# Seven block products for eight in a part of the feed-forward products of a hybrid decoder layer

## The chip, the cores and the metric

The kernel runs on one core of a Trainium2 chip. The metric is the device time of one launch in microseconds (us), the median of the runs shown. Where a profiled execution is quoted, its times count from the start of its span.

## What is computed

One layer on 256 tokens of width 2048, all in float32: a feed-forward half step (FFN1, 5632 inner columns), a mixing step (one input projection, a causal convolution over 31 taps, differential attention, one output projection), cross-attention into 256 memory tokens, and a second feed-forward half step (FFN2). Cut to what matters here:

```python
def rms_norm(x, g):
    xf = x.astype(jnp.float32)
    y = xf * lax.rsqrt(jnp.mean(xf * xf, axis=-1, keepdims=True) + EPS)
    return (y * g.astype(jnp.float32)).astype(x.dtype)

def swiglu(h, w_gate, w_up, w_down):
    return (jax.nn.silu(h @ w_gate) * (h @ w_up)) @ w_down
...
        x = x + 0.5 * swiglu(rms_norm(x, ffn1_norm_g[l]), ffn1_w_gate[l], ffn1_w_up[l], ffn1_w_down[l])
        h = rms_norm(x, mix_norm_g[l])
        p = h @ w_in[l]
...
        x = x + jnp.concatenate([o_diff, o_conv], axis=-1) @ w_out[l]
        x = x + memory_cross_attention(rms_norm(x, xattn_norm_g[l]), rms_norm(mem, mem_norm_g[l]),
                                       xattn_w_q[l], xattn_w_kv[l],
                                       xattn_q_norm_g[l], xattn_k_norm_g[l], xattn_w_o[l])
        x = x + 0.5 * swiglu(rms_norm(x, ffn2_norm_g[l]), ffn2_w_gate[l], ffn2_w_up[l], ffn2_w_down[l])
```

## The kernel before

**A weight product.** TensorE multiplies at reduced precision, so every float32 operand is split in two parts: hi (a rounded copy, `h`) and lo (what is left, `l`). A product of 128 rows of weights takes three passes, hi x hi (line 186), hi x lo (187) and lo x hi (189). Tokens are the stationary operand (two blocks of 128, `tb`), 512 columns of weights the moving one.

**A quad.** `proj` goes through two column slices (`j`) and both token blocks at once, in four accumulators of 128 x 512 in PSUM (`acc00` to `acc11`). It takes the weights in pairs of 128-row tiles. Per pair: one transfer of 512 KB per column slice (line 172, issued on SyncE's queue), a split of each (line 136, the cast on ScalarE; line 137, the subtraction on VectorE), and 2 x 2 x 2 x 3 = 24 products. In the last pair of a quad each accumulator's products stand together, so that the accumulators end one after the other, and `evac` empties them. The raw weights have 4 buffers, `wh` and `wl` 5 each, in one pool `wp` for the whole program: when TensorE has used a tile, the next split may start, and the one after it is loaded.

**Feed-forward.** The 5632 inner columns are 11 slices of 512, in groups of 4, 4 and 3. Per slice there is one *in-quad* (gate and up are the two column slices, 16 row tiles, so 8 pairs), then silu (line 289, ScalarE) and the multiplication to `h` (291, VectorE). Two steps later (`later(2, turn)`) TensorE transposes `h` (297), and it is split again into `hth` (299) and `htl` (300). After a group come two *down-quads*, each over 1024 of the 2048 output columns, 8 pairs in a group of four and 6 in the group of three; their sums are added to x (line 311).

**Between phases.** When a column group of x is final, ScalarE squares it (197), TensorE transposes it 8 times (208, a *turn*), ScalarE scales the result with the gains (`xh`, 211) and VectorE takes the lo part (`xl`, 212). A turn is put off by one or two weight steps with `later`.

**Memory tokens.** `mem_group` loads 512 columns of the memory, squares them, loads them transposed, and splits them with the gains: `mh` (218, ScalarE) and `ml` (219, VectorE), 16 of each. It is done in FFN1, at weight steps 12, 18, 24 and 30.

**Order.** Each engine runs its queue in order. The order within a queue is set at build time by a scheduler that follows the program order with the priorities and estimates it has; `later` and `behind` steer it. Convolution taps (721, 724) fill VectorE's queue wherever there is room in mixing.

## Time and profile before

| | |
|---|---|
| median of 3 runs | 1926.21 us (1925.92 to 1926.83) |
| span of the profiled execution | 1923.9 us |
| TensorE (PE) busy | 1911.3 us, 99% |
| VectorE (DVE) busy | 1095.0 us, 57% |
| ScalarE (ACT) busy | 879.1 us, 46% |
| transferred | 364.70 MB, 190 GB/s |

The span is that of one execution under the profiler; about 2.3 us lie around it. FFN1 fills it to 741, mixing to about 1060, cross-attention to 1190, FFN2 the rest. A row of the timeline is: start, duration, engine, line of the kernel, operation, what it writes and reads, and in brackets how long the engine stood idle before and what released it. Matmuls are pipelined: what one costs is the distance between starts, not its duration.

### The profile page before, as it was taken

To read this page: it belongs to the slowest core of one execution; us is meant where nothing else is said; L and a number is where in the kernel's file an instruction comes from. 1 tells how busy PE (TensorE), PEld (TensorE's weight loads), DVE (VectorE), ACT (ScalarE), POOL (GpSimd) and SP (SyncE) were. 2 spreads that over 40 slices of the span, in tenths; PEclk is the share of its full clock that TensorE was granted. 3 is DMA by queue.
4 is the path that set the end of the run, shared out by engine and by line. 5 is a ranking of instruction groups with operands and counts; after the bars stand their busy time and mean duration, and the time that the engine had idled before them with its cause. 6 is when DMAs were issued, how large, how long until landed. Compare 5 with 4: busy or idle time off the path is not lost.

```text
span 1923.9 us, 22869 instructions
## 1 busy us (share of the span) xinstructions
PE 1911.3 (99%) x8650; PEld 1579.1 (82%) x8650; DVE 1095.0 (57%) x1430; ACT 879.1 (46%) x1173; POOL 20.7 (1%) x29
## 2 busy tenths in 40 slices
...
GB/s 297 257 211 200 192 196 186 187 196 187 190 193 195 188 185 182 190 190 189 171 129 129 198 177 144 185 196 187 186 196 197 188 185 195 193 187 190 195 186 155
DMA packets 188815, 364.70 MB, mean 190 GB/s; under 512 B 11680, under 2 KB 12192, under 8 KB 188704
## 3 DMA queue, kind: packets, MB, share of 16 engines
...
HBM read 361.09 MB, written 2.10 MB: 189 GB/s over the span
## 4 chain that ended last, share of the span: by engine, by line
PE 87%; DVE 8%; DMA 2%; issue 1%; ACT 1%; POOL 0%; SPq 0%; DVEq 0%; ACTq 0%
PE acc L186 28%; PE acc L189 28%; PE acc L187 28%; DVE y L724 3%; DVE wl L137 3%; PE tp L297 1%; DMA raw<-ffn_w_up 1%; DMA raw<-ffn_w_gate 1%; PE tp L208 1%; ACT wh L136 1%; DMA raw<-w_out 0%; DVE nb L591 0%; DVE qms L536 0%; DVE uT L741 0%; DVE uT L730 0%
## 5 line engine op out<-in xcount | busy, mean ns | idle before, releaser
L137 DVE TENSOR_TENSOR wl<-raw,wh 128x1024 fp32r<-128x1024 f32 (+1 forms) x674 | 800.7, 1217 | 759.1 <-ACT wh L136 757.8
L136 ACT CAST wh<-raw 128x1024 fp32r<-128x1024 f32 (+1 forms) x674 | 682.2, 1049 | 953.3 <-PE acc L189 917.0
L186 PE MATMUL acc<-wh,xh_f 128*128 128x512 f32 x1408 | 550.5, 392 | 2.3 <-ACT s L289 2.0
L187 PE MATMUL acc<-wl,xh_f 128*128 128x512 f32 x1408 | 549.0, 390 | 0.5 <-DVE wl L137 0.4
L189 PE MATMUL acc<-wh,xl_f 128*128 128x512 f32 x1408 | 450.1, 390 | 0.0
L186 PEld LDWEIGHTS acc<-wh,xh_f 128*128 128x128 f32 x1408 | 264.9, 188 | 58.4 <-ACT s L289 2.4
L187 PEld LDWEIGHTS acc<-wl,xh_f 128*128 128x128 f32 x1408 | 265.0, 188 | 56.3 <-DVE wl L137 2.1
L189 PEld LDWEIGHTS acc<-wh,xl_f 128*128 128x128 f32 x1408 | 264.6, 188 | 55.0
L186 PE MATMUL acc<-wh,hth 128*128 128x512 f32 x704 | 274.8, 390 | 0.0
L187 PE MATMUL acc<-wl,hth 128*128 128x512 f32 x704 | 273.9, 389 | 0.0
L189 PE MATMUL acc<-wh,htl 128*128 128x512 f32 x704 | 224.6, 389 | 0.0
L189 PEld LDWEIGHTS acc<-wh,htl 128*128 128x128 f32 x704 | 132.1, 188 | 27.5
L186 PEld LDWEIGHTS acc<-wh,hth 128*128 128x128 f32 x704 | 132.2, 188 | 27.2
L187 PEld LDWEIGHTS acc<-wl,hth 128*128 128x128 f32 x704 | 132.2, 188 | 27.1
L186 PE MATMUL acc<-wh,xh_mix 128*128 128x512 f32 x320 | 125.4, 392 | 0.0
L187 PE MATMUL acc<-wl,xh_mix 128*128 128x512 f32 x320 | 124.6, 389 | 0.0
L189 PE MATMUL acc<-wh,xl_mix 128*128 128x512 f32 x320 | 101.9, 389 | 0.0
L724 DVE SCALAR_TENSOR_TENSOR y<-uT,cw,y 128x256 f32<-128x256 f32 x240 | 100.6, 469 | 0.1
L189 PEld LDWEIGHTS acc<-wh,xl_mix 128*128 128x128 f32 x320 | 60.1, 188 | 12.6
L186 PEld LDWEIGHTS acc<-wh,xh_mix 128*128 128x128 f32 x320 | 60.1, 188 | 12.3
L187 PEld LDWEIGHTS acc<-wl,xh_mix 128*128 128x128 f32 x320 | 60.1, 188 | 12.1
L291 DVE SCALAR_TENSOR_TENSOR h<-acc,rstd_f,s 128x512 f32<-128x512 f32 x44 | 32.8, 748 | 33.1 <-PE acc L189 32.0
...
## 6 DMA issues: line engine op xcount, KB each, us to landing
...
```

The source lines that it names most:

```text
L136: last[:] = [S.copy(out=wh, in_=raw), V.tensor_tensor(out=wl, in0=raw, in1=wh.bitcast(F32), op=ALU.subtract)]
L137: V.tensor_tensor(out=wl, in0=raw, in1=wh.bitcast(F32), op=ALU.subtract)]
L186: T.matmul(acc[tb][j], hs, wt[k, j][0], start=(fresh and k == 0), stop=False)
L187: T.matmul(acc[tb][j], hs, wt[k, j][1], start=False, stop=False)
L189: T.matmul(acc[tb][j], ls, wt[k, j][0], start=False, stop=(ending and k == nk - 1))
L208: T.transpose(tp[:, b, tb * P:(tb + 1) * P], srcs[tb][:, c * P:(c + 1) * P], ident)
L291: V.scalar_tensor_tensor(out=h, in0=acc[1], scalar=norm.rs(tb), in1=s, op0=ALU.mult, op1=ALU.mult)
L297: T.transpose(tp[:, i, :], h[:, i * P:(i + 1) * P], ident)
L724: V.scalar_tensor_tensor(out=yc, in0=u[:, j:j + 256], scalar=cw[:, j * 8 + ct:j * 8 + ct + 1], in1=yc, op0=ALU.mult, op1=ALU.add)
```

## The change

Two (or one) of the pairs of a feed-forward quad are computed in the manner of Strassen's scheme as Winograd arranged it. Seen as blocks, a pair is a product of a 2 x 2 matrix of token blocks (two token blocks, two 128-row tiles) with a 2 x 2 matrix of weights (two row tiles, two column slices): eight block products. In a *seven pair* there are seven, each with its three passes, so 21 matmuls for 24. They need sums of weights (lines 245, 247, 248, written over the raw weights, then split like weights: four pairs of `wh`/`wl` tiles instead of two, one of them half used) and sums of tokens (`token_sums`: four subtractions of 128 x 128, a cast `sh` and a subtraction `sl`). Two of the products go only into extra PSUM tiles (`p1`, `q6`, in the two banks of `tpp` used for transposes) and two into `q57`, two banks that the attention's pool `atp` had for the whole program and that are now opened per phase. After the last seven pair of a quad, `middle` combines them (`p1s`, `us`, `vw`, and `ys` in in-quads). In an in-quad, each accumulator is then added to its share (`full`, line 441) before silu and `h`; in a down-quad the shares are added to x directly (line 476, five operations).

Seven pairs are: pairs 1 and 3 of all in-quads but the very first; in the down-quads two pairs in groups of four (positions 3 and 5 of the order) and one in groups of three (position 3). There are 42 + 20 = 62 of them. The transposes of `h` come seven steps later instead of two, but for the last slice of a group.

The weight pool is made per phase: `wf` in the feed-forward (3 raw tiles of 1 MB, each for one pair of both column slices, 7 of `wh` and `wl`), `wm` in between with the sizes of before. The memory's preparation moves into mixing, to its weight steps 6, 12, 18 and 24. The sums for the normalised x (`row_sums`, copies at line 317) are made with the turns.

```diff
+RAWS, SPLITS = 3, 7
+S_IN = (1, 3)
+ORDER_0 = tuple(range(8))
+ORDER_IN = (0, 1, 2, 3, 4, 5, 6, 7)
+S_DOWN = {4: 2, 3: 1}
+ORDER_DOWN = {4: (1, 3, 4, 0, 5, 2, 6, 7), 3: (1, 3, 2, 0, 4, 5)}
...
-    wp = ctx.enter_context(tc.tile_pool(name="wp", bufs=5))
     xtp = ctx.enter_context(tc.tile_pool(name="xtp", bufs=4))
+    xsp = ctx.enter_context(tc.tile_pool(name="xsp", bufs=len(S_IN)))
-    atp = ctx.enter_context(tc.tile_pool(name="atp", bufs=2, space=PSUM))
...
+    def passes(acc, hs, ls, w, start, stop):
+        T.matmul(acc, hs, w[0], start=start, stop=False)
+        T.matmul(acc, hs, w[1], start=False, stop=False)
+        T.matmul(acc, ls, w[0], start=False, stop=stop)
+    def quad(parts, srcs, middle, evac, first=False):
+        acc = [[accp.tile([P, 512], F32, tag=f"acc{tb}{j}", name=f"acc{tb}{j}") for j in range(2)]
+               for tb in range(2)]
+        begun = set()
+        seven = [i for i, p in enumerate(parts) if p()[4]]
+        q = None
+        for n, part in enumerate(parts):
+            h, l, i0, row, sums = part()
+            raw = ph["w"].tile([P, 4, 512], F32, tag="raw", name="raw", bufs=RAWS)
+            wa, wb = split_tiles(), split_tiles()
...
+                nc.sync.dma_start(out=raw[:, 0:4:3, :], in_=rows_pair(srcs[0], row))
+                nc.sync.dma_start(out=raw[:, 1:3, :], in_=rows_pair(srcs[1], row))
+                split(raw[:, 0:2, :], *wa)
+                if sums:
+                    split(raw[:, 3, :], wb[0][:, 1, :], wb[1][:, 1, :])
+                else:
+                    split(raw[:, 2:4, :], *wb)
+            ev0, ev1, od1, od0 = [tuple(t[:, c, :] for t in w) for w in (wa, wb) for c in range(2)]
+            def at(b, tb):
+                return [t[:, i0 + b, tb * P:(tb + 1) * P] for t in (h, l)]
+            if sums:
+                V.tensor_tensor(out=raw[:, 1:3, :], in0=raw[:, 1:3, :], in1=raw[:, 2:4, :], op=ALU.add)
+                V.tensor_tensor(out=raw[:, 3, :], in0=raw[:, 3, :], in1=raw[:, 1, :], op=ALU.add)
+                V.tensor_tensor(out=raw[:, 0, :], in0=raw[:, 0, :], in1=raw[:, 3, :], op=ALU.add)
+                wc, wd = split_tiles(), split_tiles()
+                split(raw[:, 1:3, :], *wc)
+                split(raw[:, 0:4:3, :], *wd)
+                t3, t1, t4, t2 = [tuple(t[:, c, :] for t in w) for w in (wc, wd) for c in range(2)]
+                sh, sl = sums
+                def s(c):
+                    return [t[:, c, :] for t in (sh, sl)]
+                if q is None:
+                    q = {"p1": tpp.tile([P, 512], F32, tag="tp", name="p1"),
+                         "q6": tpp.tile([P, 512], F32, tag="tp", name="q6"),
+                         "q57": ph["q"].tile([P, 2, 512], F32, tag="q57", name="q57")}
+                st, sp = n == seven[0], n == seven[-1]
+                passes(acc[0][0], *at(0, 0), ev0, "00" not in begun, False)
+                passes(acc[0][1], *s(3), ev1, "01" not in begun, False)
+                passes(q["p1"], *at(1, 0), od0, st, sp)
+                passes(q["q57"][:, 1, :], *s(2), t3, st, sp)
+                passes(q["q57"][:, 0, :], *s(0), t1, st, sp)
+                passes(acc[1][0], *at(0, 1), t4, "10" not in begun, False)
+                passes(q["q6"], *s(1), t2, st, sp)
+                begun |= {"00", "01", "10"}
+                if sp:
+                    middle(q)
+            else:
+                ending = n == len(parts) - 1
+                wt = [[ev0, ev1], [od0, od1]]
+                for tb in range(2):
+                    for js in ([[0], [1]] if ending else [[0, 1]]):
+                        for b in range(2):
+                            hs, ls = at(b, tb)
+                            for j in js:
+                                T.matmul(acc[tb][j], hs, wt[b][j][0], start=f"{tb}{j}" not in begun, stop=False)
+                                begun.add(f"{tb}{j}")
+                                T.matmul(acc[tb][j], hs, wt[b][j][1], start=False, stop=False)
+                            for j in js:
+                                T.matmul(acc[tb][j], ls, wt[b][j][0], start=False, stop=(ending and b == 1))
+                    if ending:
+                        evac(tb, acc[tb])
+            step()
...
+    def combine(q, pool):
+        p1 = pool.tile([P, 512], F32, tag="p1", name="p1s", bufs=1)
+        S.copy(out=p1, in_=q["p1"])
+        u = pool.tile([P, 512], F32, tag="u", name="us", bufs=1)
+        V.tensor_tensor(out=u, in0=q["q6"], in1=p1, op=ALU.subtract)
+        vw = pool.tile([P, 2, 512], F32, tag="vw", name="vw", bufs=1)
+        V.tensor_tensor(out=vw, in0=q["q57"], in1=u.unsqueeze(1).broadcast_to([P, 2, 512]), op=ALU.add)
+        return p1, vw
+    def token_sums(pool, bufs, o0, e0, o1, e1):
+        s = ph["f"].tile([P, 4, P], F32, tag="sraw", name="sraw", bufs=1)
+        V.tensor_tensor(out=s[:, 0, :], in0=o1, in1=e1, op=ALU.subtract)
+        V.tensor_tensor(out=s[:, 2, :], in0=o1, in1=o0, op=ALU.subtract)
+        V.tensor_tensor(out=s[:, 1, :], in0=o0, in1=s[:, 0, :], op=ALU.subtract)
+        V.tensor_tensor(out=s[:, 3, :], in0=e0, in1=s[:, 1, :], op=ALU.subtract)
+        sh = pool.tile([P, 4, P], F32R, tag="sh", name="sh", bufs=bufs)
+        sl = pool.tile([P, 4, P], F32R, tag="sl", name="sl", bufs=bufs)
+        S.copy(out=sh, in_=s)
+        V.tensor_tensor(out=sl, in0=s, in1=sh.bitcast(F32), op=ALU.subtract)
+        return sh, sl
+    def row_sums(raws, g):
+        f = ph["f"].tile([P, 2, 256], F32, tag="xsf", name="xsf", bufs=1)
+        for c in range(2):
+            S.activation(out=f[:, c, :], in_=raws[c], func=AF.Copy, scale=col(g + c))
+        return token_sums(xsp, len(S_IN), f[:, 1, 0:P], f[:, 0, 0:P], f[:, 1, P:], f[:, 0, P:])
...
+            if pair:
+                pair(a, tp)
...
+        def pair(self, i, raws):
+            if i in self.wanted:
+                self.sums[i] = row_sums(raws, self.g0 + 2 * i)
+        def parts(self, order, seven):
+            return [lambda i=i: (*(self.grp[i // 2] or (None, None)), 2 * (i % 2), 2 * i,
+                                 i in seven and self.sums.get(i, True)) for i in order]
...
+        with tc.tile_pool(name="wf", bufs=SPLITS, reuse_waits="tile") as wf, \
+                tc.tile_pool(name="ffn", bufs=2, reuse_waits="tile") as fp, \
+                tc.tile_pool(name="qp", bufs=1, space=PSUM) as qp:
+            ph.update(w=wf, f=fp, q=qp)
...
+                    def middle(q, rest=rest):
+                        p1, vw = combine(q, fp)
+                        y = fp.tile([P, 512], F32, tag="y", name="ys", bufs=1)
+                        V.tensor_tensor(out=y, in0=vw[:, 0, :], in1=q["q57"][:, 1, :], op=ALU.add)
+                        rest.update({(0, 0): (p1, ALU.add), (0, 1): (vw[:, 0, :], ALU.add),
+                                     (1, 0): (vw[:, 1, :], ALU.subtract), (1, 1): (y, ALU.add)})
+                    def evac(tb, acc, c=c, rest=rest, end=(c == c0 + ng - 1), pairs=(c - c0 < s_down)):
+                        acc = list(acc)
+                        for j in range(2):
+                            if rest:
+                                t = fp.tile([P, 512], F32, tag="full", name="full")
+                                V.tensor_tensor(out=t, in0=acc[j], in1=rest[tb, j][0], op=rest[tb, j][1])
+                                acc[j] = t
...
-                        later(2, turn)
+                            if pairs:
+                                if tb == 0:
+                                    hold[c] = fp.tile([P, 2, 2, P], F32, tag="hold", name="hold", bufs=1)
+                                f = hold[c]
+                                S.copy(out=f[:, tb], in_=tp[:, 0:2, :])
+                                if tb:
+                                    hsums[c] = token_sums(fp, max(S_DOWN.values()), f[:, 0, 1, :], f[:, 0, 0, :],
+                                                          f[:, 1, 1, :], f[:, 1, 0, :])
+                        later(2 if end else 7, turn)
+                    quad(norm.parts(ORDER_0 if start else ORDER_IN, sevens),
+                         [wg[:, c * 512:(c + 1) * 512], wu[:, c * 512:(c + 1) * 512]], middle, evac, first=start)
...
+                    def middle(q, n0=n0):
+                        p1, vw = combine(q, fp)
+                        for tb, j, t, f in ((0, 0, p1, 0.5), (0, 1, vw[:, 0, :], 0.5), (1, 0, vw[:, 1, :], -0.5),
+                                            (1, 1, vw[:, 0, :], 0.5), (1, 1, q["q57"][:, 1, :], 0.5)):
+                            xt = X[tb][n0 + j]
...
-                    kst = [(hts[c][0], hts[c][1], i, c * 4 + i) for c in range(c0, c0 + ng) for i in range(4)]
-                    proj(kst, [wd[:, n * 512:(n + 1) * 512] for n in (n0, n0 + 1)], evac)
+                    parts = [lambda c=c0 + i // 2, a=i % 2, i=i: (*hts[c], 2 * a, c * 4 + 2 * a,
+                                                                  a == 0 and i // 2 < s_down and hsums[c])
+                             for i in ORDER_DOWN[ng]]
+                    quad(parts, [wd[:, n * 512:(n + 1) * 512] for n in (n0, n0 + 1)], middle, evac)
...
+        n1.pair(i, [raw[:, c, :] for c in range(2)])
...
-    memp = ctx.enter_context(tc.tile_pool(name="memp", bufs=1))
+    mids = ctx.enter_context(ExitStack())
+    ph["w"] = mids.enter_context(tc.tile_pool(name="wm", bufs=5, reuse_waits="tile"))
+    memp = mids.enter_context(tc.tile_pool(name="memp", bufs=1, reuse_waits="tile"))
+    atp = mids.enter_context(tc.tile_pool(name="atp", bufs=2, space=PSUM))
...
+        m = ph["w"].tile([P, 2, 512], F32, tag="raw", name="memraw", bufs=4)
+        nc.sync.dma_start(out=m, in_=mem[:, n * 512:(n + 1) * 512].rearrange("(b p) n -> p b n", p=P))
...
-        later(12 + 6 * n, lambda n=n: mem_group(n))
+        later(6 + 6 * n, lambda n=n: mem_group(n))
...
+    mids.close()
```

**VectorE, one in-quad of FFN2.** `wl` are the subtractions of the split, `h` and `htl` as above. Before:

```order
682 L137 TENSOR_TENSOR wl<-raw,wh 128x1024 x13
683 L291 SCALAR_TENSOR_TENSOR h<-acc_13934,rstd_f_9641,s 128x512
684 L291 SCALAR_TENSOR_TENSOR h<-acc_13936,rstd_f_9641,s 128x512
685 L137 TENSOR_TENSOR wl<-raw,wh 128x1024 x3
686 L300 TENSOR_TENSOR htl<-tp,hth 128x4x128 x2
```

After, the end of an in-quad and the start of the next with its first seven pair:

```order
1057 L441 TENSOR_TENSOR full<-acc_11145,vw 128x512
1058 L446 SCALAR_TENSOR_TENSOR h<-full,rstd_f_10142,s 128x512
1059 L441 TENSOR_TENSOR full<-acc_11146,vw 128x512
1060 L441 TENSOR_TENSOR full<-acc_11147,ys 128x512
1061 L150 TENSOR_TENSOR wl<-raw,wh 128x1024
1062 L446 SCALAR_TENSOR_TENSOR h<-full,rstd_f_10142,s 128x512
1063 L150 TENSOR_TENSOR wl<-raw,wh 128x1024
1064 L245 TENSOR_TENSOR raw<-raw 128x1024
1065 L150 TENSOR_TENSOR wl<-raw,wh 128x512
1066 L247 TENSOR_TENSOR raw<-raw 128x512
1067 L248 TENSOR_TENSOR raw<-raw 128x512
1068 L150 TENSOR_TENSOR wl<-raw,wh 128x1024
```

The 13 and 3 subtractions of a quad have got the adds of the weights and of the accumulators among them; each `h` stands behind the two `full` of its token block.

**ScalarE, the program's start.** `xh` are the rows of x times the gains, the casts of 512 the first pair's weights in halves, those of 1024 the next pair's. Before:

```order
6 L136 CAST wh<-raw 128x512 x2
7 L218 ACTIVATE xh_f_108<-x_78,gT 128x256 x2
8 L136 CAST wh<-raw 128x1024 x2
9 L218 ACTIVATE xh_f_110<-x_82,gT 128x256 x2
10 L136 CAST wh<-raw 128x1024 x2
```

After:

```order
6 L149 CAST wh<-raw 128x512 x2
7 L345 ACTIVATE xh_f_105<-x_75,gT 128x256 x2
8 L317 ACTIVATE xsf<-x_75,gT 128x256 x2
9 L309 CAST sh<-sraw 128x512
10 L149 CAST wh<-raw 128x1024 x2
11 L345 ACTIVATE xh_f_107<-x_79,gT 128x256 x2
```

The copies `xsf` and the cast `sh` of the token sums, which VectorE makes from `xsf`, stand ahead of the second pair's casts.

**ScalarE, from cross-attention to FFN2.** `junk` are the squares, `xh` the third group (9552) and the fourth (9618) of the normalised x; the casts are FFN2's. Before:

```order
351 L197 ACTIVATE junk,ssq_f_8876<-x_78 128x512
352 L136 CAST wh<-raw 128x1024
353 L197 ACTIVATE junk,ssq_f_8876<-x_79 128x512
354 L136 CAST wh<-raw 128x1024
355 L197 ACTIVATE junk,ssq_f_8876<-x_82 128x512
356 L211 ACTIVATE xh_f_9552<-tp,gT 128x256
357 L197 ACTIVATE junk,ssq_f_8876<-x_83 128x512
358 L211 ACTIVATE xh_f_9552<-tp,gT 128x256 x3
359 L136 CAST wh<-raw 128x1024
360 L211 ACTIVATE xh_f_9618<-tp,gT 128x256 x2
```

After (third group 10045, fourth 10119; row 459 holds the first casts of FFN2):

```order
450 L322 ACTIVATE junk,ssq_f_9345<-x_75 128x512
451 L317 ACTIVATE xsf<-tp,gT 128x256 x2
452 L322 ACTIVATE junk,ssq_f_9345<-x_76 128x512
453 L322 ACTIVATE junk,ssq_f_9345<-x_79 128x512
454 L309 CAST sh<-sraw 128x512
455 L336 ACTIVATE xh_f_10045<-tp,gT 128x256
456 L322 ACTIVATE junk,ssq_f_9345<-x_80 128x512
457 L336 ACTIVATE xh_f_10045<-tp,gT 128x256 x3
458 L336 ACTIVATE xh_f_10119<-tp,gT 128x256 x3
459 L149 CAST wh<-raw 128x1024 x2
```

Before, FFN2's first two casts stand between the squares; now they stand behind all of them and behind seven of the eight `xh`. On TensorE the turn of the fourth group, which stood behind FFN2's first 24 products, now stands ahead of them, next to that of the third. From FFN1 to mixing it is alike.

## Rows read from the trace of the kernel before

**Rows 1.** The page: engine table, and the costliest line of products.

```profile
PE 1911.3 (99%) x8650; PEld 1579.1 (82%) x8650; DVE 1095.0 (57%) x1430; ACT 879.1 (46%) x1173; POOL 20.7 (1%) x29
...
L186 PE MATMUL acc<-wh,xh_f 128*128 128x512 f32 x1408 | 550.5, 392 | 2.3 <-ACT s L289 2.0
```

**Rows 2.** The waits: who waited for whom, us in total, times, longest us.

```profile
ACT wh L136 <- PE acc L189: 917.0, 293, 5.4
```

**Rows 3.** Windows: stretch, length, busy us (count) by engine, granted clock, DMA share, GB/s.

```profile
0.00:60.00 60.00, 56.05 (x223) 42.52 (x224) 35.40 (x57) 36.54 (x59) 1.99 (x10) 0.97 0.90 304
...
400.00:800.00 400.00, 400.00 (x1806) 332.07 (x1805) 200.46 (x202) 169.97 (x202) 1.10 (x3) 1.00 0.61 190
...
860.00:940.00 80.00, 80.00 (x357) 66.26 (x356) 80.00 (x157) 36.87 (x43) 0.00 (x0) 1.00 0.61 190
940.00:1004.00 64.00, 61.74 (x330) 50.15 (x328) 61.64 (x153) 47.63 (x118) 4.02 (x4) 1.00 0.47 143
1004.00:1040.00 36.00, 35.00 (x188) 28.82 (x187) 26.65 (x53) 28.22 (x76) 6.79 (x6) 1.00 0.38 120
```

**Rows 4.** Timeline of a steady in-quad of FFN1: start, duration, engine, what.

```profile
600.16 0.39 PE L186 MATMUL acc<-wh,xh_f 128*128 128x512 f32 x1
...
600.38 0.39 PE L187 MATMUL acc<-wl,xh_f 128*128 128x512 f32 x1
...
602.58 2.36 DVE L137 TENSOR_TENSOR wl<-raw,wh 128x1024 fp32r<-128x1024 f32 x2 [3.08 <-ACT wh L136]
...
606.93 2.01 ACT L136 CAST wh<-raw 128x1024 fp32r<-128x1024 f32 x2 [3.43 <-PE acc L189]
```

**Rows 5.** Instructions by line and shape: count, busy us, mean ns, idle before.

```profile
L137 DVE TENSOR_TENSOR wl<-raw,wh 128x1024 fp32r<-128x1024 f32 x670 | 797.9, 1220 | 757.7 <-ACT wh L136 756.5
L136 ACT CAST wh<-raw 128x1024 fp32r<-128x1024 f32 x670 | 679.8, 1052 | 951.7 <-PE acc L189 917.0 <-DVE y L724 10.3 <-DMA raw<-ffn_w_gate 8.1
...
L706 DVE TENSOR_TENSOR x<-acc,x 128x512 f32<-128x512 f32 x16 | 10.7, 682 | 0.2 <-PE acc L189 0.2
...
L219 DVE SCALAR_TENSOR_TENSOR ml<-rawm,gT,mh 128x256 fp32r<-128x256 f32 x16 | 6.9, 478 | 0.0
...
L834 ACT COPY pT<-tp 128x512 f32<-128x512 f32 x4 | 2.1, 590 | 0.7 <-PE tp L831 0.7
...
L542 DVE TENSOR_TENSOR rot<-qk,ropeB 128x128 f32<-128x128 f32 x4 | 1.1, 278 | 0.0
```

**Rows 6.** Timeline of the start: the second pair's first cast on ScalarE.

```profile
9.74 1.05 ACT L136 CAST wh<-raw 128x1024 fp32r<-128x1024 f32 x1 [0.44 <-DMA raw<-ffn_w_gate]
```

**Rows 7.** Timeline from FFN1 to mixing: cast, turn, last sum of x.

```profile
740.03 1.05 ACT L136 CAST wh<-raw 128x1024 fp32r<-128x1024 f32 x1 [0.68 <-ACT junk L197]
...
741.15 1.03 PE L208 MATMUL tp<-ident,x 128*128 128x128 f32 x8
...
742.26 0.68 DVE L311 SCALAR_TENSOR_TENSOR x<-acc,x 128x512 f32<-128x512 f32 x1
```

**Rows 8.** Timeline from cross-attention to FFN2: turn, cast, last x, square, xh.

```profile
1189.85 1.03 PE L208 MATMUL tp<-ident,x 128*128 128x128 f32 x8
...
1190.27 1.03 ACT L136 CAST wh<-raw 128x1024 fp32r<-128x1024 f32 x1
1190.43 0.68 DVE L861 TENSOR_TENSOR x<-acc,x 128x512 f32<-128x512 f32 x1
...
1191.21 0.63 ACT L197 ACTIVATE junk<-x 128x512 bf16<-128x512 f32 x1
...
1192.80 0.82 ACT L211 ACTIVATE xh_f<-tp,gT 128x256 fp32r<-128x256 f32 x2
...
1194.76 0.48 ACT L211 ACTIVATE xh_f<-tp,gT 128x256 fp32r<-128x256 f32 x1 [1.14 <-DVE xl_f L212]
```

**Rows 9.** Timeline of VectorE around the convolution's end: channel sum, mean taken off.

```profile
1004.82 3.87 DVE L730 TENSOR_REDUCE uT<-y 128x256 f32<-128x2048 f32 x1
...
1040.57 1.22 DVE L734 TENSOR_TENSOR y<-y,pm 128x1024 f32<-128x1024 f32 x1 [2.32 <-PE pm L732]
```

101 lines of the change are left out of this document (53 added, 48 removed).

## Prediction

> **What bounds the kernel now.** The page's engine table comes first: TensorE is busy 1911.3 of the span of 1923.9 us, VectorE 57% of it, ScalarE 46% [rows 1]. The waits say the same from the other side: ScalarE's casts spend 917.0 us waiting for TensorE to give back a weight buffer [rows 2], and TensorE, over 1408 products of the feed-forward layers, loses 2.3 us [rows 1]. So fewer products shorten the kernel by their own length, as long as the weights are split in time and the accumulators are emptied in time. The windows show where that holds with room to spare: in FFN1 VectorE works half the time (200.46 us of 400), but in 860 to 940, under the convolution, it is full [rows 3]. The timeline of a steady quad gives the step: the products start 0.22 us apart at 600, and ScalarE's casts, one step of two per weight pair, take 2.01 us and wait 3.43 [rows 4], so a pair lasts 5.44 us. 5.44 / 24 products = 0.2267 us each.
>
> By the Trainium skill, TensorE: Matmul & The Clock Gate (Part 1), such a product takes 215.7 ns; the trace has 226.7. With the page's figure the gain below would be 40.1 instead of 42.2 us; the trace's step is used.
>
> **The gain.** A seven pair issues 21 products for 24. The in-quads (gate and up) have two each, 21 of them (all but the first): 42. The down quads have two in the groups of four and one in those of three: 8 x 2 + 4 x 1 = 20. 62 x 3 = 186 products, x 0.2267 = **-42.2 us**. The three passes of a block product go into one accumulator in a row, as the last pair of every quad does already, at the same step.
>
> **What it adds.** A plain pair costs VectorE two subtractions in 2.36 us [rows 4]. A seven pair costs three of 1024 and one of 512, one add of 1024 and two of 512. An operation of two tensors of 512 has a row at 0.68; the add of 1024, which has none, is taken as the subtraction of that size, 1.22 (1.18 each where two follow) [rows 4, 5]: 3 x 1.18 + 0.68 + 1.22 + 2 x 0.68. That makes 6.8 us. An in-quad is then: 6 x 2.36 = 14.2; 2 x 6.8 = 13.6; the combination (512, 1024, 512) 2.6; the emptying, four adds and two h, 6 x 0.68 = 4.1; two htl 1.4; the token sums, four of 128 at 0.28 and one of 512, 1.8. Together **37.7 us, against 6 x 5.44 + 2 x 4.76 + 1.0 of transposes = 43.2 us of TensorE**. ScalarE: 12 casts at 1.05, 2 x (3 x 1.05 + 0.6) for the seven pairs, and some 5 of silu, hth and copies: 25 us. VectorE would be 87% full, so TensorE stays the bound on the average of a quad. All additions make about 480 us of VectorE and 140 of ScalarE, in the shadow of TensorE.
>
> The average is not enough; two deadlines stand inside a quad. *Slots.* Seven split slots, four of them taken by a seven pair, so that the second seven pair's last three splits wait until the first one's products let slots go. The first of these is free 6 products (1.4 us) into that pair; TensorE then needs 3.4 us for its rest and 5.4 for the plain pair between: 8.8 us, in which VectorE has 6.8 - 1.2 = 5.6 us to do. Spare: 3 us. *Accumulators.* They end 1.36 us apart and the next quad asks for each one 4.1 us after its end; the add that empties it takes 0.68 us. It is queued on VectorE behind subtractions of 1.2 us, which leaves about 1 to 2 us. Both hold by the rows, but a quad has some 20 hand-overs more than before. I allow **+2 us** in all (0.06 a quad); the bounds are 0 and 10 us (0.3 us in each of 33 quads, a cast that comes one hand-over late).
>
> **The start.** On ScalarE and VectorE the sums of pair 1 now stand between the x rows and the casts of pair 1: two copies of 256 (0.82 for two such [rows 8]), four subtractions of 128 (1.1), one cast of 512 (0.6). The copies and that cast stand on ScalarE before the cast of 9.74 us [rows 6], with the subtractions between them: 9.74 becomes about 12.2, once. TensorE has no work in hand there: **+2.3 us** (0 if the weights of pair 1 came that much later anyway, 3.4 with an ml-sized step and a hand-over more).
>
> **FFN1 to mixing.** The weight pools change here. Before, the first cast of w_in (740.03) comes ahead of the last squares, and TensorE goes from a turn of 8 transposes at 741.15 (1.03 us) straight to products at 742.2; the other turn follows them [rows 7]. After, the cast stands behind the squares and four xh of the third group, and both turns, 16 transposes, come first. From the last x (742.26 + 0.68): the square and its hand-over 0.8, xh 4 x 0.41, the cast 1.05 (prices in [rows 5, 8]) bring the first product from 742.2 to about 745.5. Of these 3.5 us the second turn, 1.03, is work that had to be done anyway, and the wl of the second column comes 0.6 later: **+3.1 us** (0 to 4.2).
>
> **Cross-attention to FFN2.** The same, worse. Before, FFN2's second cast is at 1190.27, ahead of the last square, and products follow the third turn at 1190.9 [rows 8]. After, the first cast stands behind all squares, the sums of pairs 1 and 3, and seven xh. From the last x (1190.43 + 0.68 [rows 8]): the square and its hand-over 0.8, seven xh at 0.41 = 2.9, the change between ScalarE, VectorE and TensorE over the two transpose banks 0.9 (ScalarE waits 1.14 there now [rows 8]), the cast 1.05: 1196.8. 1196.8 - 1190.9 less the turn 1.03 = 4.9, and 0.6 for the second column's wl: **+5.5 us** (0 to 7). The weights themselves arrive in time: their buffers are new, and their transfers wait only for the last split of w_o.
>
> **Memory tokens.** 16 ml (0.478 each [rows 5]) move from FFN1, where VectorE is idle half the time, into mixing. A quarter of them comes before 800; the other 12 x 0.478 = 5.7 us fall where VectorE is full. They delay the convolution, whose sum ends at 1008.7, while its mean on TensorE is used at 1040.6 [rows 9], and in 1004 to 1040 VectorE has 36.0 - 26.65 = 9.4 us free [rows 3]; what is delayed with it are splits and attention steps in 940 to 1004, where TensorE already loses 2.3 us [rows 3]. **+2 us** (0 to 5.7). The ScalarE half and the squares lie in idle time (36.87 of 80 busy [rows 3]); the transfers are only moved.
>
> **Sum.** -42.2 + 2 + 2.3 + 3.1 + 5.5 + 2 = -27.3 us. The profiled execution's span was 1923.9, 2.3 below the median of 1926.2 (time outside the span, unchanged): about 1896.6 of span and **1898.9 us**.
>
> **Rivals.**
> (a) *VectorE's queue becomes the bound in the seven pairs.* For: in-order queue, 87% full, four slots of seven. Against: 3 us spare per seven pair, and all its prices have rows. It decides from the point where the adds and hand-overs of a seven pair cost 3 us more than the rows; each 0.44 us beyond that, in 62 pairs, costs 27.3 us, the whole gain. With 1 us late per pair: 1899 + 62 = 1961 us; with 0.2 us, 1911. I give 8% to the part that ends slower, 12% to a partial loss at 1905 to 1922.
> (b) *The boundaries cost nothing*, because a cast overtakes in reality what the order shows behind it, or the products start on earlier data: -42.2 + 2 + 2 = 1888. Against: queues keep their order. 13%.
> (c) *The gain in full and the boundaries at their upper ends*: +3.4 + 4.2 + 7 + 5.7 + 2 instead of 14.9: 1906. 13%.
> (d) *The clock falls after the gaps.* In before TensorE's granted clock is 0.97 over the first 60 us, where it starts at the lower level (1.2 GHz) after standing idle, and 1.00 in the steady stretches [rows 3]: 0.03 x 60 = 1.8 us of full clock were missing at the start. The idle gaps at the boundaries, about 2.5 and 5 us, are longer than any that the steady stretches can hold; a fall like the start's costs 1.8 us each, 1901 to 1903. 12%.
> By the Trainium skill, TensorE: Matmul & The Clock Gate (Part 1), an idle stretch does bring the half rate back; no row of before shows a fall.
> (e) *The seven pairs don't run faster*: each product waits for its own load of the tokens, which neighbours used to share. Against: every product has a load of its own already (8650 to 8650 [rows 1]). 2%, 1926 or over.
>
> **How the numbers follow.** My forecast has 40%, (a) 20 (of it 8 slower, 2 within, 10 faster), (b) 13, (c) 13, (d) 12, (e) 2. Faster by over 0.2% (3.9 us, about what a measurement of this kernel can tell from no change): 40 + 10 + 13 + 13 + 12 = 0.88. Within 0.2%: 2 of (a) and (e) = 0.04. Slower: 0.08. The forecast's own steps reach from 1890 to 1908 by their bounds taken one or two at a time; the range takes in (b), (c), (d) and half of the partial (a): 1887 to 1915.
>
> **What would show it.** Right: products 0.2267 us apart in seven pairs, 3 x 62 fewer; TensorE near 99% still, VectorE near 1575 us, ScalarE near 1020; one idle gap of TensorE of about 2.5 us after FFN1 and one of about 5 before FFN2, each ended by a cast. Wrong: idle time of TensorE in every quad, ended by VectorE's subtraction (slots) or by its adds to accumulators (a); no gaps at the boundaries (b); a granted clock below 1.00 after 60 us (d).

## The result and the profile after

The changed kernel takes **1902.3 us** in the median (1900.64 to 1903.71, 4 runs), beside 1926.07 us (1924.41 to 1926.83, 4 runs) for the kernel before: ratio 0.9876, 95% interval 0.9862 to 0.989, so 23.8 us faster. The forecast was 1898.9 with a range of 1887 to 1915. The profiled execution took 1900.64 us, its span is 1898.9 us against 1923.9: 25.0 us shorter.

The page of the changed kernel: the engine table (busy us, share, instructions), to be read beside [rows 1], and the first line of the chain that ended last, which had PE at 87% and DVE at 8% before:

```profile
PE 1874.4 (99%) x8464; PEld 1545.5 (81%) x8464; DVE 1543.1 (81%) x2041; ACT 1034.8 (54%) x1372; POOL 23.7 (1%) x29
...
PE 84%; DVE 11%; DMA 2%; ACT 1%; issue 1%; POOL 1%; SPq 0%; DVEq 0%; ACTq 0%
```

TensorE has 186 products fewer (8650 to 8464) and still stands at 99%. VectorE went from 57% to 81%. The waits of the changed kernel (who waited for whom: us, times, longest) answer to [rows 2]:

```profile
ACT wh L149 <- PE acc L285: 381.7, 302, 5.5
...
ACT wh L149 <- DVE raw L245: 82.8, 34, 5.6
```

ScalarE now waits for the weight additions too (L245), but most of its waiting is still for TensorE to give slots back: the products set the pace. The windows (stretch, length, busy us and count by engine, granted clock, DMA) of a stretch of steady quads and of three stretches outside them answer to [rows 3]:

```profile
400.00:600.00 200.00, 200.00 (x892) 165.89 (x891) 165.09 (x174) 103.39 (x110) 0.00 (x0) 1.00 0.61 200
860.00:940.00 80.00, 78.17 (x360) 63.99 (x359) 79.74 (x161) 40.41 (x54) 0.00 (x0) 1.00 0.62 191
1004.00:1040.00 36.00, 32.48 (x166) 26.65 (x166) 29.98 (x48) 23.95 (x52) 4.04 (x3) 1.00 0.39 123
1150.00:1200.00 50.00, 45.59 (x204) 36.93 (x204) 36.17 (x59) 30.50 (x58) 0.70 (x1) 0.93 0.36 117
```

In the quads TensorE is busy all the time, with VectorE at 83%. What was lost lies outside them: at the start (see below), under the convolution and around the entry of FFN2, where the clock is below 1.00 too.

The starts of TensorE's instructions on the timeline cut every profiled execution into the same parts. The table gives them for all kernels of this study, in us: the last product of FFN1; from there to the first product of mixing; from FFN1's last product to the convolution's mean (`pm`); from FFN1's last product to the last product of w_o (the middle); from that one to FFN2's first product; and from w_o's last product to the end. The first, the middle and the last but one add up to the span.

| kernel | FFN1 ends | mixing starts | pm | middle | FFN2 starts | w_o to end | span |
|---|---|---|---|---|---|---|---|
| before | 740.92 | +1.02 | +299.02 | 448.70 | +1.02 | 734.28 | 1923.9 |
| after | 723.68 | +4.39 | +305.63 | 455.38 | +7.32 | 719.84 | 1898.9 |
| e4_plain | 742.64 | +4.39 | +305.54 | 455.52 | +6.95 | 741.04 | 1939.2 |
| e5_dve2 | 724.04 | +4.38 | +306.50 | 456.19 | +7.49 | 720.27 | 1900.5 |
| e6_dve4 | 727.62 | +3.72 | +307.92 | 457.65 | +6.88 | 720.33 | 1905.6 |
| e1_order_f2 | 725.10 | +4.39 | +306.02 | 455.70 | +1.61 | 715.70 | 1896.5 |
| e2_order_both | 723.48 | +1.02 | +304.07 | 453.76 | +1.61 | 715.76 | 1893.0 |
| e3_mem_one | 722.97 | +4.39 | +302.21 | 451.90 | +7.98 | 719.93 | 1894.8 |
| e9_order_start | 725.59 | +1.02 | +303.86 | 453.56 | +1.61 | 716.65 | 1895.8 |
| e7_three | 722.59 | +4.39 | +306.68 | 456.41 | +6.44 | 717.50 | 1896.5 |
| e11_order_three | 720.74 | +1.02 | +302.73 | 452.42 | +1.61 | 716.64 | 1889.8 |
| e12_order_gp | 725.03 | +1.02 | +311.72 | 461.41 | +1.61 | 716.16 | 1902.6 |
| e13_all | 720.91 | +1.02 | +312.51 | 462.06 | +1.61 | 715.93 | 1898.9 |
| e14_turn_late | 720.25 | +1.02 | +303.11 | 452.79 | +1.60 | 708.86 | 1881.9 |

Before to after: FFN1 -17.2, middle +6.7, FFN2 -14.4. The 30 seven pairs of FFN1 are worth 30 x 0.68 = 20.4 us and the 32 of FFN2 21.8. So FFN1 lost 3.2 us of its gain and FFN2 7.3. The steady quads lost nothing: from the third in-quad's first silu to the last in-quad's, ScalarE's timeline has 140.09 to 669.59 before and 141.87 to 654.98 after, 16.4 us less, for 24 seven pairs of 0.68 = 16.3 us between them.

The timeline of the changed kernel at the entry of FFN2, TensorE and the two casts (start, duration, engine, line, idle before and its releaser):

```profile
1179.06 0.39 PE L188 MATMUL acc<-wh,oxl 128*128 128x512 f32 x1
...
1182.80 1.72 PE L333 MATMUL tp<-ident,x 128*128 128x128 f32 x8 [2.47 <-DVE xl_f L337]
...
1185.28 1.99 ACT L149 CAST wh<-raw 128x1024 fp32r<-128x1024 f32 x2
...
1186.38 2.07 PE L281 MATMUL acc<-wh,xh_f 128*128 128x512 f32 x4 [1.86 <-ACT wh L149]
...
1188.25 1.06 PE L283 MATMUL acc<-wl,xh_f 128*128 128x512 f32 x2
...
1190.57 0.63 PE L283 MATMUL acc<-wl,xh_f 128*128 128x512 f32 x2
```

The last product of w_o starts at 1179.06, FFN2's first at 1186.38, released by a cast that stood behind all the squares, the sums and seven xh. The first pair's weights had landed long before, at 1168.98 and 1170.83. Then four products take 2.07 us and two take 1.06: they are 0.43 us apart, half speed, until 1190.4, and two take 0.63 again after that. In 1180 to 1190 the granted clock is 0.67 (a row of it stands in the last section).

### The profile page after: what moved, and what is told of

It reads as the page before. It is cut to its first block, busy times and chain, and to the rows that moved or that the text cites. A ratio compares the mean times of both kernels' runs of the same rounds, so it can differ in the third digit from the quotient of the medians.

```text
span 1898.9 us, 23191 instructions
## 1 busy us (share of the span) xinstructions
PE 1874.4 (99%) x8464; PEld 1545.5 (81%) x8464; DVE 1543.1 (81%) x2041; ACT 1034.8 (54%) x1372; POOL 23.7 (1%) x29
## 4 chain that ended last, share of the span: by engine, by line
PE 84%; DVE 11%; DMA 2%; ACT 1%; issue 1%; POOL 1%; SPq 0%; DVEq 0%; ACTq 0%
PE acc L283 19%; PE acc L281 19%; PE acc L285 19%; DVE y L905 4%; DVE wl L150 4%; PE acc L188 3%; PE acc L186 3%; PE acc L185 3%; PE acc L199 2%; PE q L199 2%; PE acc L200 2%; PE q L200 2%; PE acc L201 2%; PE q L201 2%; PE tp L452 1%
## 5 line engine op out<-in xcount | busy, mean ns | idle before, releaser
L149 ACT CAST wh<-raw 128x1024 fp32r<-128x1024 f32 (+1 forms) x798 | 798.7, 1016 | 730.0 <-PE acc L285 381.7
L150 DVE TENSOR_TENSOR wl<-raw,wh 128x1024 fp32r<-128x1024 f32 (+1 forms) x798 | 930.4, 1178 | 301.6 <-ACT wh L149 278.2
L281 PE MATMUL acc<-wh,xh_f 128*128 128x512 f32 x1072 | 420.4, 394 | 5.0 <-ACT wh L149 3.2
L283 PE MATMUL acc<-wl,xh_f 128*128 128x512 f32 x1072 | 418.4, 392 | 1.1 <-DVE wl L150 1.1
L285 PE MATMUL acc<-wh,xl_f 128*128 128x512 f32 x1072 | 346.2, 391 | 0.0
L283 PEld LDWEIGHTS acc<-wl,xh_f 128*128 128x128 f32 x1072 | 202.1, 189 | 44.6 <-DVE wl L150 3.6
L245 DVE TENSOR_TENSOR raw<-raw 128x1024 f32<-128x1024 f32 x62 | 75.6, 1220 | 0.5
L199 PE MATMUL q<-wh,sh 128*128 128x512 f32 x186 | 72.5, 390 | 0.0
L201 PE MATMUL q<-wh,sl 128*128 128x512 f32 x186 | 72.4, 389 | 0.0
L200 PE MATMUL q<-wl,sh 128*128 128x512 f32 x186 | 72.4, 389 | 0.0
```

Source lines behind the costliest of these rows:

```text
L149: last[:] = [S.copy(out=wh, in_=raw), V.tensor_tensor(out=wl, in0=raw, in1=wh.bitcast(F32), op=ALU.subtract)]
L150: V.tensor_tensor(out=wl, in0=raw, in1=wh.bitcast(F32), op=ALU.subtract)]
L199: T.matmul(acc, hs, w[0], start=start, stop=False)
L200: T.matmul(acc, hs, w[1], start=False, stop=False)
L201: T.matmul(acc, ls, w[0], start=False, stop=stop)
L281: T.matmul(acc[tb][j], hs, wt[b][j][0], start=f"{tb}{j}" not in begun, stop=False)
```

## Experiments

**The seven pairs alone.** This kernel keeps the changed frame and order but computes all eight pairs plainly.

```
- n1 = Norm(G_FFN1, "f1", S_IN)      + n1 = Norm(G_FFN1, "f1")      (n4 likewise)
- sevens = () if start else S_IN     + sevens = ()
- S_DOWN = {4: 2, 3: 1}              + S_DOWN = {4: 0, 3: 0}
```

> The changed kernel with no seven pair at all: new pools, new tiles, memory tokens in mixing, the late turns, but 24 products for every pair and no sums. Theory (62 seven pairs are worth 42.2 us with no loss in the quads, 3.2 us of the loss at the start and some 1.5 at FFN2's entry come from the sums, the rest from boundaries and memory): 1902.3 + 42.2 - 4.7 = about 1940 us, slower than before by 14. Rival (seven pairs lose part of their gain in the quads and the frame costs less): 1926 to 1932 us.

Measured: 1941.47 us (1940.98 to 1945.6), ratio to before 1.0085 [1.0066, 1.0104]. Between this kernel and the changed one lie 39.2 us, the worth of the seven pairs with their sums, against 42.2 by counting steps. The frame without them is 15.3 us slower than before: the table has +1.7 in FFN1, +6.8 in the middle, +6.8 from w_o's end to the end. So of the 17.2 us that the changed kernel loses, all but about 2 belong to the frame (pools, layout, order, memory), not to the seven pairs. Even of these 2, the 1.5 in FFN1 (3.2 less 1.7) can't be put down to the sums: behind TensorE's wait for the first quad's silu the clock falls in before and in the changed kernel, and doesn't in e4_plain, and one such fall costs 1.7 us (last section).

**VectorE's room in the seven pairs (rival a).** Two, and in another kernel four, additions of 512 on VectorE are put ahead of the slots' use in every seven pair; they only keep VectorE busy.

```
+ for _ in range(2):                        # 4 in e6_dve4
+     V.tensor_tensor(out=pad, in0=pad, in1=pad, op=ALU.add)
  wc, wd = split_tiles(), split_tiles()
```

> Two idle adds of 512 elements on VectorE, on a tile that nothing else uses, in each of the 62 seven pairs, between the sums of the weights and their splits: 1.3 us more per pair, 80 us of VectorE in all. Theory (the second seven pair's splits have 3 us to spare, and VectorE's 165 us of 200 in a steady stretch become 177): no change, 1900 to 1904 us, TensorE still without idle time from 60 to 700. Rival (VectorE's queue is already what sets the quads, and the steady stretches are full only by chance): up to 1.3 x 62 = 80 us more, 1920 to 1980 us.

> Four such adds in each seven pair: 2.6 us, 160 us in all. Theory: the spare of 3 us is nearly used up and VectorE stands at 189 us of 200 in a steady stretch, so it just holds or begins to give: 1902 to 1912 us. Rival (the margin of the accumulators, some 1 us, decides, not that of the slots): 1 us or more lost in each of 33 quads, 1930 us and over.

Measured: 1902.42 us (1902.08 to 1902.9), ratio 0.9881 [0.9867, 0.9896], and 1906.71 us (1903.87 to 1907.69), ratio 0.9901 [0.9886, 0.9916]. The group of the added work in e5_dve2 (count, busy us, mean ns, idle before), and windows of 200 us inside FFN1 of e5_dve2 and then of e6_dve4:

```profile
L252 DVE TENSOR_TENSOR pad<-pad 128x512 f32<-128x512 f32 x124 | 85.6, 691 | 1.6
```

```profile
200.00:400.00 200.00, 200.00 (x891) 165.35 (x890) 197.49 (x241) 101.13 (x114) 0.00 (x0) 1.00 0.59 200
```

```profile
200.00:400.00 200.00, 199.81 (x888) 164.51 (x886) 196.77 (x239) 101.59 (x114) 0.00 (x0) 1.00 0.59 200
```

1.4 us more in each of 62 seven pairs costs nothing in the median, with VectorE busy 99% of the stretch and TensorE never idle. 2.8 us more cost 4.4 us in all, which is 0.07 us for each of 62 pairs; TensorE just begins to wait (199.81). By the table, e6_dve4's profiled execution is 6.7 us longer than the changed kernel's: 3.9 in FFN1, 2.3 in the middle, which has no seven pair, and 0.5 in FFN2. FFN1's part is real: from the third in-quad's first silu to the last's it takes 516.5 us instead of 513.1, and behind the down-quads TensorE waits for VectorE to empty accumulators:

```profile
531.74 0.47 PE L285 MATMUL acc<-wh,xh_f 128*128 128x512 f32 x1 [0.46 <-DVE x L485]
```

FFN2, with 32 of the pairs, shows no such loss. So the room is a little under 3 us for each pair, and rival (a) did not happen.

**The order at the two boundaries.** The squares and the turns of the third and fourth group of x are put behind the first weights of the next stage, as the kernel before had them; first for FFN2 alone, then for mixing as well.

```
  def after_x(norm, tb, n):
+     if norm.name == "f2" and n >= 2:      # e2_order_both: in ("f2", "mix")
+         if tb == 1:
+             def rest():
+                 with behind(list(last)):
+                     for b in range(2):
+                         norm.sq(b, n)
+                     norm.turn(n)
+             later(n, rest)
+             if n == 3:
+                 later(n, norm.finish)
+         return
      norm.sq(tb, n)
```

> At the entry of FFN2 only: the squares and turns of the third and fourth column group of x are put off until after FFN2's first weight pair and are issued behind its splits. Nothing is left out. Theory (the queue's order costs the time: the weights landed some 10 us earlier, and the cast stood behind squares, sums and seven xh): the first FFN2 product follows the last w_o product within 1 us instead of 7.3, the granted clock does not fall there, and the 7.1 us lost at this place go: about 1895 us against 1902.3. Rival (the new pool's buffers or the transfers set the start, whatever the order): the cast stays where it is, 1902 us. Rival (the clock falls at this place anyway, for a reason other than the gap): only the 4.3 us of idle time go, 1898 us, and the granted clock of 1150 to 1200 stays near 0.93.

> The same at both boundaries, FFN1 to mixing and cross-attention to FFN2. Theory: another 3.4 us go at the first boundary (idle 2.1 before the second turn and 0.5 before a subtraction), about 1892 us. Rival (the first boundary's loss is the wait of the new weight pool for buffers of the old one): 1895 us, as without it, with the first cast of w_in still after 726 us of the span.

Measured: 1897.68 us (1896.45 to 1899.86), ratio 0.9852 [0.9837, 0.9867]; and 1896.61 us (1894.74 to 1898.99), ratio 0.9846 [0.983, 0.9861]. TensorE's timeline of e2_order_both at the entry of FFN2, where w_o's last product starts at 1177.24:

```profile
1178.85 0.73 PE L281 MATMUL acc<-wh,xh_f 128*128 128x512 f32 x2 [0.34 <-ACT wh L149]
1180.14 0.73 PE L283 MATMUL acc<-wl,xh_f 128*128 128x512 f32 x2 [0.57 <-DVE wl L150]
...
1185.29 0.39 PE L199 MATMUL acc<-wh,xh_f 128*128 128x512 f32 x1
...
1189.00 0.50 PE L199 MATMUL acc<-wh,xh_f 128*128 128x512 f32 x1 [0.94 <-ACT wh L149]
```

The gap is gone and so is the half speed: the first seven pair starts 8.05 us after w_o's end (1185.29) instead of 14.69 (1193.75 in the changed kernel), 6.6 us earlier. Of these 4.1 are left at the end (719.84 to 715.76). The remaining turn (1.1 us) now lies behind the first products, and the first seven pair itself takes longer, with 0.94 us of wait for a cast.

At mixing the first product comes 3.37 us earlier too, but `pm` only 2.0 us earlier against e1_order_f2, or 1.6 against the changed kernel. In the median e2_order_both is only 1.1 us faster than e1_order_f2, less than the 4 us over which its runs scatter. The products of mixing aren't what its middle waits for. Windows of e2_order_both under the convolution:

```profile
860.00:940.00 80.00, 77.90 (x358) 63.97 (x358) 80.00 (x163) 39.98 (x57) 0.00 (x0) 1.00 0.60 186
```

VectorE is full there before [rows 3], after (79.74 of 80) and here, while TensorE, still full before, is not in the two later ones (78.17 and 77.90). A start that comes earlier on TensorE's side is given back in part before VectorE's last tap.

**The memory tokens.** Only the first of the four groups of memory is prepared; the other three groups use the first one's tiles, and their transfers, squares, mh and ml are left out.

```
- for n in range(4):
-     later(6 + 6 * n, lambda n=n: mem_group(n))
+ later(6, mem_all)          # mem_group(0), then mgrp[1..3] = mgrp[0]
```

> Three of the four groups of memory tokens are not prepared (no loads, squares, mh, ml; the first group stands for all four), so cross-attention computes something else. Theory (12 ml and what belongs to them cost 3.2 us in mixing, because VectorE is full there and attention's steps stand behind them): mixing gets 3 us shorter, about 1899 us. Rival (mixing lost its 3 us to another order of attention and convolution, which the scheduler made because of the new pools): no change, 1902 us.

Measured: 1898.59 us (1896.58 to 1899.9), ratio 0.9854 [0.984, 0.9869]; the middle is 3.5 us shorter than in the changed kernel, 3.4 of it before `pm`. Preparing the memory in mixing costs about that much, where 2 us were forecast. The experiment takes ScalarE's half and the transfers away with VectorE's 12 ml, so it doesn't say which of them costs it.

**The start.** To both orders above, the sums of pairs 1 and 3 are moved behind the casts that follow the first quad's rows, and the part of x that goes into the tile of pair 3's rows is loaded a step later.

```
- n1.pair(i, [raw[:, c, :] for c in range(2)])
+ if i in S_IN:
+     later({1: 3, 3: 1}[i], lambda: behind_last(lambda: n1.pair(i, [raw[:, c, :] for c in range(2)])))
- later(i - AHEAD + 1, lambda spot=spot: load_x(*spot))
+ later(i - AHEAD + (2 if i == 3 else 1), lambda spot=spot: load_x(*spot))
```

> The order of both boundaries as in the earlier run that changed both, and at the program's start the token sums of pairs 1 and 3 put off by three and one weight steps, behind the splits of that step (one load of x later by one step for it). Theory (the start lost 3.2 us, of which 1.4 by the sums: the kernel without seven pairs reaches FFN1's end 1.4 us earlier than the changed one when its 30 pairs are counted at 0.68 us): 1896.6 - 1.4 = about 1895 us, and the second pair's cast on ScalarE back from 12.1 to about 10 us. Rival (the transfers set the start, since the second pair's weights land at 10 us and the later ones late as well): no change, 1896 to 1897 us.

Measured: 1896.51 us (1894.09 to 1897.59), ratio 0.9846 [0.983, 0.9863]: no gain over e2_order_both in the median, where runs of each scatter over 3.5 us and more. ScalarE's timeline at the second pair's first cast, in the changed kernel, in this one and in e4_plain:

```profile
11.57 0.62 ACT L309 CAST sh<-sraw 128x512 fp32r<-128x512 f32 x1 [1.09 <-DVE sraw L306]
12.09 1.99 ACT L149 CAST wh<-raw 128x1024 fp32r<-128x1024 f32 x2
```

```profile
11.87 1.99 ACT L149 CAST wh<-raw 128x1024 fp32r<-128x1024 f32 x2 [2.64 <-DMA raw<-ffn_w_up]
```

```profile
11.61 2.00 ACT L149 CAST wh<-raw 128x1024 fp32r<-128x1024 f32 x2 [1.79 <-DMA raw<-ffn_w_up]
```

With the sums out of the way, ScalarE waits 2.64 us for the transfer of ffn_w_up and casts only 0.22 us earlier. e4_plain, which has no sums at all, casts at 11.61 and waits 1.79 for the same transfer. Before, the first cast took the gate rows alone (9.74, [rows 6]); in the new layout a cast covers a gate row and an up row, and so waits for both transfers. The up rows landed at 11.07 before, at 11.46 in the changed kernel, 11.59 in e4_plain and 11.85 here; so the sums held the changed kernel's cast back by 0.6 us, and the layout did the rest.

**A third seven pair.** If VectorE still has room, a third of the eight pairs of every in-quad but the first can be a seven pair: 21 more, 14.3 us by steps. Tried on the changed kernel, and then with both orders put back.

```
- S_IN = (1, 3)
+ S_IN = (1, 3, 5)
```

> A third seven pair (5) in each in-quad but the first, with its sums at the start and at FFN2's entry. 21 more pairs, 14.3 us less of TensorE. Theory (VectorE's 35.5 us of 43.1 in an in-quad become 40.4 of 42.4, still under the bound, and the sums at the entries cost about 1 us): about 1889 us. Rival (three pairs that take four of seven slots each, with one plain pair between, leave VectorE behind): the gain is lost or turned, 1900 us and over, with idle time of TensorE in the in-quads ended by subtractions.

> Changed kernel with the order of both boundaries put back (squares and turns of the third and fourth group behind the first weights of mixing and of FFN2) and a third seven pair in every in-quad but the first. Apart they measured 1896.6 and 1895.9 against 1902.3 of the changed kernel. If what they win lies at different places (boundaries; steady quads), they add up: 1902.3 - 5.7 - 6.4 = about 1890. Rival: at the entry of FFN2 the sums of three pairs instead of two stand on VectorE, so that the order's 6.6 us there mostly go again: 1894 to 1896.

Measured: 1895.87 us (1892.75 to 1898.29), ratio 0.9846 [0.9832, 0.9861]; with the order 1891.4 us (1889.55 to 1891.88), ratio 0.9821 [0.9805, 0.9838]. Less than half of 14.3 us came: 6.4 and 5.2. FFN2 gained nothing over e2_order_both (716.64 against 715.76). TensorE's waits of e7_three have a new line at the top; on TensorE's timeline of e11_order_three one such wait, and the window of 10 us around it:

```profile
PE tp L452 <- DVE us L295: 5.2, 9, 2.7
```

```profile
1596.11 0.66 PE L463 MATMUL tp<-ident,h 128*128 128x128 f32 x4 [1.92 <-DVE us L295]
```

```profile
1590.00:1600.00 10.00, 8.08 (x35) 6.29 (x34) 7.68 (x9) 5.32 (x7) 0.00 (x0) 0.86 0.90 286
```

The two block products `p1` and `q6` of a quad's seven pairs live in the two transpose banks until VectorE combines them (`us`). With a third seven pair the combination falls right before the turn of the last quad's h, which needs the same banks. TensorE waits up to 2.7 us, and behind the wait shown the clock falls (0.86). Two causes were left open by this: the banks' hold, or VectorE at 95% in 1200 to 1300. The next kernel tells them apart: it is e11_order_three with the turn one pair later.

```
- later(2 if end else 7, turn)
+ later(2 if end else 8, turn)
```

> As with the order of both boundaries and three seven pairs (1891.4), but a quad's h is turned one pair later. With three seven pairs the turn came right behind the third one's products, while its two block products still held both transpose banks until VectorE had combined them: TensorE waited 5.1 us in 9 places there, 4.3 of them in FFN2, and in 1590 to 1600, behind the longest of these waits (1.92), the granted clock was 0.86. Theory (banks): the waits go and the clock with them, 1884 to 1887. Rival (VectorE's 95% in these quads is the limit, and the wait only moves to casts or accumulators): 1889 to 1893.

Measured: **1883.09 us** (1881.9 to 1884.76), ratio 0.9777 [0.976, 0.9793], the fastest of this study, 19 us under the changed kernel. The page's engine table and two windows of it:

```profile
PE 1857.9 (99%) x8401; PEld 1529.8 (81%) x8401; DVE 1625.6 (86%) x2156; ACT 1064.5 (57%) x1420; POOL 25.7 (1%) x29
```

```profile
1500.00:1600.00 100.00, 100.00 (x455) 83.07 (x454) 94.75 (x109) 59.85 (x71) 0.00 (x0) 1.00 0.63 216
1590.00:1600.00 10.00, 10.00 (x50) 8.38 (x49) 9.82 (x12) 4.90 (x7) 0.00 (x0) 1.00 0.94 309
```

The waits for `us` are gone, and the fall of the clock in 1590 to 1600 with them; VectorE has the same work (1625.6 us, 1626.7 in e11_order_three), and FFN2 is 7.8 us shorter than in e11_order_three. So it was the banks. FFN2 is 6.9 us under e2_order_both, where 11 seven pairs count for 7.5.

FFN1 did not do as well: it ends 3.2 us earlier than in e2_order_both, where 10 seven pairs count for 6.8. Of the missing 3.6, about 1 is lost before TensorE goes on behind the first silu (59.29 instead of 58.31). After it VectorE is the limit in places: in 60 to 140 it is busy for 77.4 of 80 us, and TensorE waits for its adds. The rest was not followed up.

```profile
101.85 0.47 PE L281 MATMUL acc<-wh,xh_f 128*128 128x512 f32 x1 [0.52 <-DVE full L452]
188.54 0.50 PE L281 MATMUL acc<-wh,hth 128*128 128x512 f32 x1 [0.63 <-DVE full L452]
```

**The memory's low parts on GpSimd.** VectorE's ml is replaced by two operations on GpSimd, with both orders put back, and in another kernel with three seven pairs too.

```
- hi_lo(*mgrp[n], raw[:, c, :], G_MEM + 4 * n + c, c)
+ S.activation(out=h[:, c, :], in_=raw[:, c, :], func=AF.Copy, scale=col(g))
+ G.tensor_scalar(out=raw[:, c, :], in0=raw[:, c, :], scalar1=col(g), scalar2=None, op0=ALU.mult)
+ G.tensor_tensor(out=l[:, c, :], in0=raw[:, c, :], in1=h[:, c, :].bitcast(F32), op=ALU.subtract)
```

> The order of both boundaries put back, and the low parts of the memory tokens formed on GpSimd in two operations instead of one on VectorE. Taking three of four groups away won 3.5 us in mixing. Theory (VectorE is the bound in mixing, and its 12 low parts of 0.48 us = 5.7 us are what the middle lost): the middle falls from 453.8 to about 450.5 and the time from 1896.6 to about 1893. Rival (what cost the time was ScalarE's half and the queue order, not VectorE's work, or GpSimd slows VectorE's operations beside it): no gain, 1896 to 1900.

> Order of both boundaries, three seven pairs in every in-quad but the first, and the memory's low parts on GpSimd. If the three gains are independent: 1902.3 - 5.7 - 6.4 - 3 = about 1887. Rival: they are the same VectorE time counted more than once, or the clock falls at other gaps: 1890 to 1895.

Measured: 1904.47 us (1902.84 to 1905.15), ratio 0.989 [0.9876, 0.9905], 8 us slower than e2_order_both; and 1900.74 us (1899.19 to 1903.03), ratio 0.9873 [0.9858, 0.9888], 9 us slower than e11_order_three. The middle lost 7.7 and 9.6 us. A miss: both are slower than even the rivals allowed. In 740 to 880 of e12_order_gp, SP's waits, and in 740 to 1010 ScalarE's:

```profile
SPq L171 <- POOL ml L671: 32.5, 4, 10.0
```

```profile
ACT wh L149 <- DMA raw<-w_in: 33.0, 16, 8.4
```

The memory's raw tile is one of the four buffers of the weights' pool. GpSimd gives it back late: its two operations took 1.31 and 1.02 us for each of four parts, where VectorE took 0.48 [rows 5]. SP's queue stands up to 10 us at the next load of w_in, and the cast after it waits up to 8.4 us. In e2_order_both the same line of ScalarE has 4.0 us in all, against 33.0 here. TensorE then stands too, and in 870 to 880 the granted clock is 0.76, where e2_order_both has 1.00. VectorE's taps ran slower as well, as the rival had it. The taps' group in 780 to 960, of e12_order_gp and of e2_order_both (count, busy us, mean ns):

```profile
L920 DVE SCALAR_TENSOR_TENSOR y<-uT,cw,y 128x256 f32<-128x256 f32 x210 | 94.9, 510 | 0.0
```

```profile
L916 DVE SCALAR_TENSOR_TENSOR y<-uT,cw,y 128x256 f32<-128x256 f32 x211 | 88.8, 485 | 0.0
```

By the Trainium skill, GPSIMD Engine Reference (Specifications), GpSimd's interfaces to SBUF are shared with VectorE, and instructions of VectorE with two SBUF inputs are among those that contend for them; the taps' 25 ns agree in direction, but this run doesn't part them from other causes. How much of the 8 us is the held buffer and how much the taps was not tested either.

So the question the experiment was made for, whether VectorE's ml are the 3.5 us of the middle, stays open. A buffer of its own for the memory's raw tile would have told; it wasn't tried.

## Why the prediction came out as it did

*The gain, -42.2: right.* The page has 186 products fewer, and in the changed kernel the products of a seven pair stand 0.227 us apart on TensorE's timeline, as the plain ones do:

```profile
1193.75 0.39 PE L199 MATMUL acc<-wh,xh_f 128*128 128x512 f32 x1
1193.98 0.39 PE L200 MATMUL acc<-wl,xh_f 128*128 128x512 f32 x1
1194.20 0.39 PE L201 MATMUL acc<-wh,xl_f 128*128 128x512 f32 x1
```

*The steady quads, +2 forecast, 0 measured.* The silu times give the counted gain to 0.1 us. The allowance for late hand-overs was not needed. The spare of 3 us was worked out rightly: it is about what the padding of 1.4 us (no loss) and 2.8 us (small loss) showed, though the wait that came first was for accumulators, not for slots. VectorE was forecast at 1575 us and stands at 1543.1, ScalarE at 1020 and at 1034.8.

*The start, +2.3 forecast, 3.2 measured by FFN1's loss: size nearly right, reason wrong.* The cast came at 12.09 as worked out (12.2), but for the sums only by 0.6 us. They take time that the layout would spend waiting for the second transfer anyway: the "0 if the weights of pair 1 came that much later" was the case that nearly holds, with the wait itself new. e4_plain has 1.7 us of the loss without any sums, and without the fall of the clock at 50 to 60 that before has; with one fall's 1.7 us on top, that is the whole loss. That the size came out near was luck. The prediction followed ScalarE's queue and didn't ask which transfers the new cast needs.

*FFN1 to mixing, +3.1 forecast, 2.8 measured by the same count, but worth less.* The gap stands where it was put. It is ended not by the cast but by VectorE's low part of the first turn, behind which the second turn follows. The first product comes 3.37 us later than before; less the turn of 1.03, and with 0.50 us of wait for a wl, that is 2.8. (The prices that the prediction names add up to 746.4, not 745.5, as 742.94 + 0.8 + 1.64 + 1.05: the slip came out nearer than its own prices would have.) TensorE's timeline of the changed kernel:

```profile
723.68 0.39 PE L285 MATMUL acc<-wh,htl 128*128 128x512 f32 x1
723.91 1.03 PE L333 MATMUL tp<-ident,x 128*128 128x128 f32 x8
727.05 1.26 PE L333 MATMUL tp<-ident,x 128*128 128x128 f32 x8 [2.10 <-DVE xl_mix L337]
728.07 0.70 PE L185 MATMUL acc<-wh,xh_mix 128*128 128x512 f32 x2
```

What failed is the step that added it to the memory term as if both were TensorE's time. e2_order_both takes the 3.37 us away and wins 1.6 of them in the middle, where VectorE is full under the convolution.

*The memory, +2 forecast, about 3.5 measured.* The middle is 6.7 us longer, where the boundary and the memory together were forecast at 5.1. e3_mem_one takes 3.5 us away and the order at the boundary 1.6; which part of the frame the other 1.6 belong to stays open. The 3.5 lie within the bounds (0 to 5.7), but nearer to the upper one: the 9.4 us that VectorE had free in 1004 to 1040 hid little of the delay. That what ends last there is the chain from the last tap, and not VectorE's sum of work, is argued from VectorE's full stretch and was not tested.

*Cross-attention to FFN2, +5.5 forecast, 7.3 measured.* The late start is as forecast: FFN2's first product comes 7.32 us after the last of w_o instead of 1.02, less the turn of 1.03 that had to be done anyway, 5.3. The other 2.0 us are rival (d): the clock fell behind the gap, for some nine products, most of them 0.43 us apart instead of 0.227. e1_order_f2 and e2_order_both, which close the gap, show no fall there. The prediction gave this rival 12% and let it cost 1.8 us at each boundary: about right for the place, and for one of the two. By the Trainium skill, TensorE: Matmul & The Clock Gate (Part 1), an idle stretch brings the half rate back; the trace agrees at this gap and, as the last section shows, not at every gap of its length.

*The sum.* -42.2 + 0 + 3.2 + 6.7 (the middle) + 7.3 = -25.0 us of span, against -27.3 forecast. The errors of single terms (quads -2, start +0.9, middle +1.6, FFN2 +1.8) partly cancel: without the 2 us for the quads, which nothing needed, the forecast would have been 4.3 us off, and that they offset each other is luck. The 1902.3 us lie in what rival (d) was given, 1901 to 1903, and one of its two falls came true, so the time alone doesn't tell the forecast from (d). Rivals (b) and (e) fell: the first products behind the two boundaries come 3.4 and 6.3 us later than before, where the order of the queues said so, and the seven pairs run at full step. Rival (c) is nearest for FFN2 in size (7 us), but the clock, which it did not count on, is part of the 7.3, and its loss in the quads did not come.
